# A one-core decoder step: where the near keys are copied, how wide the dense matmuls are, and how the weights lie

## The chip, the core and the metric

The kernel runs on one core of a Trainium2 chip. Its engines are TensorE (PE, with its weight loads as PEld), VectorE (DVE), ScalarE (ACT), GpSimd (POOL) and SyncE (SP); the last mainly issues DMAs, which all run on the core's 16 DMA engines. The metric is the device time of one launch in microseconds (us); arranging the inputs on the host before the launch is not in it.

## What is computed

One layer of a hybrid decoder, in float32, for a prompt of 1024 tokens and for 8 sequences of 8 new tokens (64 sample tokens) that have a cache of 2048 keys and values each:

```python
h = rmsnorm(x, norm_mix)
proj = h @ w_in                          # 1024 -> 3592 columns
a = gated_delta_rule(conv(proj[q, k, v]))     # 4 heads, with gates from 8 columns of w_in
b = dilated_window_attention(proj[q, k, v])   # 8 heads; sample tokens read the cache
x = x + concat(norm(a) * silu(z), norm(b)) @ w_out
h = rmsnorm(x, norm_ffn)
x = x + (silu(h @ w_gate) * (h @ w_up)) @ w_down     # width 2816
y = rmsnorm(x, norm_final)
```

Besides y it returns new states and caches. new_wk_sample is the key cache of each sequence, moved on by 8 rows: 2040 old rows and 8 new ones, 8 x 4 MB.

## The kernel before

Every dense product is made of three matmuls: each operand is split into a high part (ACT copies it, L223) and a low part (DVE subtracts, L224), and hi x hi, lo x hi and hi x lo are added in PSUM. wload (L226) fetches 512 KB of a weight on SP's queue into one of two raw buffers (WB = 2), wsplit makes whi and wlo, of which there are three each (WL = WH = 3), or, with own, four pairs in another pool. dense_T (L309) makes 128 output columns of all tokens, 24 matmuls per chunk of tokens; nat_mm (L1153) keeps 128 tokens in place and streams the weight.

The tokens come in two halves: F = 0 has four tiles of 128 prompt tokens, F = 1 has four more and the 64 sample tokens. The work is written as generators that yield an estimate of PE time, and beside() deals out the instructions of a main generator and of a side one by these; a scheduler then orders each engine's instructions by priority and readiness, and every queue runs in its order. keep_in_program_order pins a DMA behind the previous instruction of its queue.

The order of the stages is: norm and w_in projections (proj_a, proj_b) with the delta rule beside them; attention over the first half, outproj_a, and the first two pairs of decode_k; then the first half's outproj_b, ffn_norm and ffn(0) as the main work ("dense"), beside them attn(1), decode_k for the last two pairs, and decode_v; then outproj_b(1), ffn_norm(1) and ffn(1) with far_rows beside, which copies the far values in HBM (1536 KB each).

What the change touches: at the start (L1412 to L1417) two x tiles are loaded, then the table of constants (with the identity that the transposes use), the weight wmix, the first w_in weight, and three x tiles. Weights are sliced from their row-major arrays, so a 128-column weight tile arrives in pieces of 512 bytes, a 256-column one in pieces of 1 KB. Inside decode_k, at L1026, POOL's queue copies the last 512 keys of a sequence from cache to output, 1 MB. outproj_b works in four slices of 256 columns, one weight tile each. ffn takes its hidden blocks nb at a time (4, and 2 at f = 0 of F = 1 and at f = 20 of F = 0), gate and up by dense_T in chunks of tokens (512 for F = 0; 288 and 288 for F = 1), then the down projection: for F = 0 in four slices of 256 columns, for F = 1 in two of 512.

Of the kernel before, what the change touches and what calls it, by code (L numbers as in the profile page):

```python
# [86 lines left out]
def consts():  # L87

    p = np.arange(128)[:, None]
    c = np.arange(128)[None, :]  # L90
    c64 = np.arange(64)[None, :]
    c8 = np.arange(8)[None, :]
    t = {}
    t["ident"] = p == c
    t["ii"] = (p % 64) == (c % 64)
    t["utri"] = p <= c
    t["ones"] = np.ones((128, 128))
    t["maskT"] = np.where(c >= p, 0.0, NEG)
# [24 lines left out]
    ln = logn(count(d))  # L123
    wb = np.stack([np.where(d >= 0, -s * d, 0.0) + ln for s in slopes]).astype(np.float32)

    tt = (np.arange(128)[:, None] % 64) // 8
    sl = slopes[np.arange(128) % 8][:, None]
    x = np.arange(512)[None, :]
    dist = np.concatenate([
        np.broadcast_to(2048 - 16 * np.arange(96)[None, :], (128, 96)),  # L130
        512 + tt - 4 * (x % 128) - x // 128,
        tt - np.arange(8)[None, :]], axis=1)
    db_all = (np.where(dist >= 0, -sl * dist, 0.0) + logn(count(dist))).astype(np.float32)

    cc = np.arange(8)[None, :, None]
    rr = np.arange(32)[None, None, :]
    xin = (rr == cc + 8 * (np.arange(128)[:, None, None] % 4)).astype(np.float32).reshape(128, 256)
    return off, {"table": table, "wb": wb, "dbias": np.ascontiguousarray(db_all), "xin": xin}


def laid_out(cache_k):

    k = cache_k[0, :, PAST - 512:].reshape(DB, 128, 4, 4, 128)
    return np.ascontiguousarray(k.transpose(0, 4, 3, 2, 1).reshape(DB, 128, 4, 512))


def body(tc, I, O, C, off):
# [25 lines left out]
    ident, ii, utri, ones = K("ident"), K("ii"), K("utri"), K("ones")  # L173
# [52 lines left out]
    def wload(src, k, n):  # L226
        raw = wp.tile([128, k, n], F32, name="wraw", tag="wraw", bufs=WB)
        sp.dma_start(raw, src)
        return raw

# [89 lines left out]
    w_in = I["w_in"].rearrange("o (k p) n -> p (o k) n", p=128)  # L320
# [3 lines left out]
    def in_cols(i):  # L324
        return w_in[:, :, i * 128:(i + 1) * 128]
# [16 lines left out]
    def proj_a(G, tp, tb, hi, lo, ready={}):  # L342
# [38 lines left out]
        sp.dma_start(raw, w_in[:, :, 2048:2056])  # L381
# [35 lines left out]
    def proj_b(G, tp, hi, lo):  # L417

        W = GW[G]
        for kind in range(4):  # L420
            for j in range(4):
                c0_ = 2056 + kind * 512 + j * 128 if kind < 3 else 1536 + j * 128
                w = wsplit(w_in[:, :, c0_:c0_ + 128], 8, 128)
# [567 lines left out]
    def decode_k(tp, pairs, kb=2, kt_=3, qb=2, pb=1):  # L991
# [23 lines left out]
        for pi in pairs:  # L1015
            S = tp.tile([96, 2, 64], F32, name="S", tag="S", bufs=1)
            pa = obank()
            for s in range(2):
                b = 2 * pi + s
                c16, o16, c4, o4, src = cache_rows(I["cache_win_k"], O["new_wk_sample"], b)  # L1020
                for j in range(4):
                    for i in range(2):
                        hs = slice(i * 64, i * 64 + 64)
                        nc.gpsimd.tensor_copy(qbd[hs, s, j, 2 * j + i::8], qf[hs, j, b * 8:(b + 1) * 8])
                n = PAST - 512
                pool_q.dma_start(O["new_wk_sample"][0, b, n - DS:PAST - DS].rearrange("(a e) h d -> a (e h d)", a=64),  # L1026
                                 I["cache_win_k"][0, b, n:PAST].rearrange("(a e) h d -> a (e h d)", a=64))
# [117 lines left out]
    w_g = I["w_gate"].rearrange("o (k p) n -> p (o k) n", p=128)  # L1145
    w_u = I["w_up"].rearrange("o (k p) n -> p (o k) n", p=128)
    w_d = I["w_down"].rearrange("o (k p) n -> p (o k) n", p=128)
# [72 lines left out]
    def outproj_b(F, tp, x2):  # L1220
# [11 lines left out]
        for c in range(4):  # L1232
            w = wsplit(w_out[:, 4:8, c * 256:(c + 1) * 256], 4, 256)
            for i, rows, col in toks(F):
                ps = mbank()[:, :256]
                nat_mm(his(hi), his(lo), w, 4, rows, col, ps, True, True)
                xv = x2[:, col // 128, c * 256:(c + 1) * 256]
                dve.tensor_tensor(xv, ps, xv, op=OP.add)  # L1238
                yield 1.3
# [21 lines left out]
    def ffn(F, tp, x2, hp):  # L1261
        cols = [(0, 288), (288, 288)] if F else [(0, 512)]
# [19 lines left out]
        while f < nf:  # L1282
# [3 lines left out]
            for j in range(nb):  # L1286
                wg = wsplit(w_g[:, :, (f + j) * 128:(f + j + 1) * 128], 8, 128)
                wu = wsplit(w_u[:, :, (f + j) * 128:(f + j + 1) * 128], 8, 128)
                for c0, n in cols:
                    pg = yield from dense_T(*wg, hi, lo, c0, n)  # L1290
                    pu = yield from dense_T(*wu, hi, lo, c0, n)
                    th = hp.tile([128, 512], F32, name="hth", bufs=2)[:, :n]
                    act.activation(th, pg[:, :n], AF.Tanh, scale=0.5)  # L1293
                    dve.scalar_tensor_tensor(th, th, 1.0, pg[:, :n], op0=OP.add, op1=OP.mult)
                    dve.tensor_tensor(th, th, pu[:, :n], op=OP.mult)
                    act.activation(hh[j][:, c0:c0 + n], th, AF.Copy, scale=0.5)
                    m = min(n, 512 - c0)
                    dve.scalar_tensor_tensor(hl[j][:, c0:c0 + m], th[:, :m], 0.5, hh[j][:, c0:c0 + m].bitcast(F32),
                                             op0=OP.mult, op1=OP.subtract)
                    if m < n:  # L1300
                        dve.scalar_tensor_tensor(hh[j][:, 576:640], th[:, m:n], 0.5, hh[j][:, 512:576].bitcast(F32),
                                                 op0=OP.mult, op1=OP.subtract)
                yield 0.1
            last, wide = f + nb == nf, F or nb == 2
            ncol = 512 if wide else 256
            parts = nb * ncol // 1024

            def weights(c):

                k = nb // parts  # L1310
                return [wsplit(w_d[:, f + q * k:f + (q + 1) * k, c * ncol:(c + 1) * ncol], k, ncol, own=hp if F else None)
                        for q in range(parts)]
# [25 lines left out]

    def far_rows(c, o, new):
# [5 lines left out]
        sp.dma_start(o[0, :, PAST - DS:PAST].rearrange("b t h d -> b t (h d)"), new.rearrange("(b t) f -> b t f", t=DS))  # L1345

# [66 lines left out]
    sp.dma_start(tab, C["table"])  # L1413
    wbc = bcast_row(npl, I["norm_mix"], "wmix")
    raws = [(i, wload(in_cols(i), 8, 128)) for i in IN_ORDER[:E1]]
    x0 += load_in(0, npl, range(2, 5))
    raws += [(i, wload(in_cols(i), 8, 128)) for i in IN_ORDER[E1:E2]]  # L1417
# [51 lines left out]
    dense = Side(outproj_b(0, hp, x2), ffn_norm(0, hp, x2), ffn(0, hp, x2, hp))  # L1469
    with ExitStack() as s1:  # L1470
# [9 lines left out]
    with ExitStack() as s1:  # L1480
        dv = Side(decode_v(pool(s1, "dv", "right")), ahead=O6)
        beside(dense, (dv, R8), until=U5)
        dv.run()
    op = pool(st1, "h1", "right")
# [39 lines left out]
```

## Time and profile before

| | us |
|---|---|
| runs, median of 3 | 1784.57 |
| lowest and highest run | 1784.05 and 1786.42 |
| the profiled execution, its own time | 1786.49 |
| its span, first to last instruction | 1784.7 |
| PE busy | 1697.0 |
| DVE busy | 1150.2 |
| ACT busy | 679.4 |

The profile is of one execution. In the timeline a row is one instruction or several merged ones: start, duration, engine, line, operation, out<-in, count, and in brackets how long the engine was idle before it and what ended that. A busy PE is not PE at its peak: the ends of matmuls are modelled and overlap, so the cost of one in a run is read from start to start. The granted clock of PE is given as a share of 2.4 GHz; its lower level is 1.2.

### The profile page before, as it was taken

Reading aid. Unit: us, or ns where it says so; the run is one execution under the profiler, and the core shown is the slowest. Engines: PE = TensorE matmul, PEld = TensorE weight load, DVE = VectorE, ACT = ScalarE, POOL = GpSimd, SP = SyncE. Lnnn points to the kernel's source line nnn. Section 1 sums busy time; section 2 is a strip of 40 time slices with the busy share of each in tenths; the row PEclk is TensorE's granted clock in tenths of the full one; section 3 lists DMA queues with packets and bytes.
Section 4 is the critical chain, followed back from the end, with each engine's and each line's share of the span. In section 5 each row is a group of like instructions: output and inputs, shape, how many; then the busy total and the mean of one; then the engine's idle time right before and its main releaser. Section 6 shows DMA issues by size and latency. Waiting matters only on the chain. (4 is left out here: it accounts for less than half of the span.)

```text
span 1784.7 us, 27958 instructions
## 1 busy us (share of the span) xinstructions
PE 1697.0 (95%) x10462; PEld 1464.7 (82%) x10462; DVE 1150.2 (64%) x2829; ACT 679.4 (38%) x1379; POOL 78.2 (4%) x200
## 2 busy tenths in 40 slices
PE   4999999997999999999999989999998999999997
PEld 4988789996766668878887778888887999999996
DVE  6978966866776757797666546676576444343435
ACT  4545434441423353676421134454234223131222
POOL 1000000001001000000011001111100000000000
PEclk9999999998999999999998999999998999999999
DMA  8645556468898867534299678798494333241321
GB/s 272 182 145 159 162 179 171 116 200 271 266 282 256 256 208 225 188 104 118 66 284 287 180 224 256 248 304 274 133 325 154 128 95 95 59 130 36 107 72 65
DMA packets 309569, 324.96 MB, mean 182 GB/s; under 512 B 28221, under 2 KB 260669, under 8 KB 307754
## 3 DMA queue, kind: packets, MB, share of 16 engines
q1 hardware_dynamic: 297754, 275.64, 51.6%
q0 software_dynamic: 10304, 43.08, 6.8%
q10 hardware_dynamic: 1376, 4.46, 0.7%
q8 instruction: 82, 1.34, 0.3%
q14 instruction: 53, 0.43, 0.1%
HBM read 251.31 MB, written 105.63 MB: 200 GB/s over the span
## 5 line engine op out<-in xcount | busy, mean ns | idle before, releaser
L198 PE MATMUL pm<-act_hi,whi 128*128 128x288 f32 (+1 forms) x1056 | 349.4, 331 | 0.2 <-ACT act_hi L223 0.2
L198 PE MATMUL pm<-act_lo,whi 128*128 128x288 f32 (+1 forms) x1056 | 348.1, 330 | 0.0
L198 PE MATMUL pm<-act_hi,wlo 128*128 128x288 f32 (+1 forms) x1056 | 347.4, 329 | 0.0
L223 ACT ACTIVATE whi<-wraw 128x1024 fp32r<-128x1024 f32 x182 | 192.8, 1059 | 381.8 <-PE pm L198 275.8
L224 DVE TENSOR_TENSOR wlo<-wraw,whi 128x1024 fp32r<-128x1024 f32 x182 | 222.3, 1222 | 123.8 <-ACT whi L223 123.3
L198 PE MATMUL pm<-xh,whi 128*128 128x320 f32 (+2 forms) x672 | 230.6, 343 | 11.5 <-ACT whi L223 8.6
L198 PE MATMUL pm<-xl,whi 128*128 128x320 f32 (+2 forms) x672 | 228.4, 340 | 0.1
L198 PE MATMUL pm<-xh,wlo 128*128 128x320 f32 (+2 forms) x672 | 226.7, 338 | 0.2
L198 PEld LDWEIGHTS pm<-act_hi,whi 128*128 128x128 f32 x1056 | 199.2, 189 | 18.4 <-issue 2.1
L198 PEld LDWEIGHTS pm<-act_hi,wlo 128*128 128x128 f32 x1056 | 199.3, 189 | 14.5 <-issue 0.5
L198 PEld LDWEIGHTS pm<-act_lo,whi 128*128 128x128 f32 x1056 | 199.3, 189 | 14.2 <-issue 0.2
L198 PEld LDWEIGHTS pm<-xh,whi 128*128 128x128 f32 x672 | 129.1, 192 | 25.9 <-ACT whi L223 9.1
L1320 DVE TENSOR_TENSOR x<-pm,x 128x256 f32<-128x256 f32 (+1 forms) x148 | 79.9, 543 | 98.2 <-PE pm L198 97.8
L198 PEld LDWEIGHTS pm<-xl,whi 128*128 128x128 f32 x672 | 129.0, 192 | 11.9 <-issue 3.2
L198 PEld LDWEIGHTS pm<-xh,wlo 128*128 128x128 f32 x672 | 128.7, 192 | 10.6 <-DVE wlo L224 1.5
L198 PE MATMUL pm<-own,hh 128*128 128x512 f32 x440 | 129.4, 390 | 0.0
L198 PE MATMUL pm<-whi,hh 128*128 128x256 f32 (+1 forms) x336 | 101.6, 303 | 12.9 <-DVE x L1320 7.6
L198 PE MATMUL pm<-whi,hl 128*128 128x256 f32 (+1 forms) x336 | 99.7, 299 | 0.0
L198 PE MATMUL pm<-wlo,hh 128*128 128x256 f32 (+1 forms) x336 | 99.4, 297 | 0.0
L198 PEld LDWEIGHTS pm<-own,hh 128*128 128x128 f32 x440 | 82.2, 188 | 16.9 <-issue 0.2
L198 PE MATMUL pm<-whi,nat_hi 128*128 128x256 f32 x288 | 83.4, 293 | 1.5 <-DVE n_ss L219 1.1
L1293 ACT ACTIVATE hth<-pm 128x288 f32<-128x288 f32 (+1 forms) x66 | 30.5, 462 | 139.4 <-PE pm L198 139.3
(362 smaller groups left out, 3180.9 us busy)
## 6 DMA issues: line engine op xcount, KB each, us to landing
wraw<-w_in SPq DMA_DIRECT2D x56, 512.0 KB, 4.6
wraw<-w_gate SPq DMA_DIRECT2D x44, 512.0 KB, 3.7
wraw<-w_up SPq DMA_DIRECT2D x44, 512.0 KB, 3.8
wraw<-w_down SPq DMA_DIRECT2D x44, 512.0 KB, 3.6
new_wk_sample<-cache_win_k SPq DMA_DIRECT2D x8, 1536.0 KB, 8.2
qbc<-smp SPq DMA_DIRECT2D x32, 384.0 KB, 7.2
kt<-cache_win_k SPq DMA_DIRECT2D x32, 384.0 KB, 7.0
vt<-cache_win_v SPq DMA_DIRECT2D x32, 384.0 KB, 4.2
```

The costliest lines, as they stand in the source:

```text
L198: pe.matmul(out, lhsT, rhs, start=start, stop=stop)
L223: act.activation(hi, src, AF.Copy)
L224: dve.tensor_sub(lo, src, hi.bitcast(F32))
L1293: act.activation(th, pg[:, :n], AF.Tanh, scale=0.5)
L1320: dve.tensor_tensor(xv, ps, xv, op=OP.add)
```

## The change

The near keys are no longer copied in decode_k. wload now takes one entry of a list after each weight load, when there is one, and issues it on SP's queue: a copy of 256 rows (512 KB), pinned behind the load. The list of 16 copies is set just before the dense work of the first half begins, and what is left of it is issued when that work's side generators are done. The identity leaves the table and gets a tensor of its own; at the start wmix, the identity, the first weight and the last three x tiles come ahead of the table. w_in, w_gate, w_up and w_down are laid out on the host so that each weight tile is one block with 4 KB per partition; w_out stays. outproj_b and the down projection of F = 0 work in two slices of 512 columns, with two weight tiles of 256 rows each per slice. The second FFN takes its tokens as 256 and 320, and in its first step goes through both hidden blocks for the first 256 tokens before it comes to the other 320; the second block's weights lie in the own buffers.

```diff
-    t["ident"] = p == c
...
+def lay_out(a):
+
+    a = dict(a)
+    a["w_ba"] = np.ascontiguousarray(a["w_in"][0][:, 2048:2056].reshape(8, 128, 8).transpose(1, 0, 2))
+    a["w_in"] = blocks_of(a["w_in"], IN_COLS)
+    for k in ("w_gate", "w_up"):
+        a[k] = blocks_of(a[k], range(0, FF, 128))
+    a["w_down"] = np.ascontiguousarray(a["w_down"][0].reshape(11, 2, 128, 2, 512).transpose(0, 3, 2, 1, 4))
+    return a
...
-    ident, ii, utri, ones = K("ident"), K("ii"), K("utri"), K("ones")
+    ident = cp.tile([128, 128], F32, name="ident")
+    ii, utri, ones = K("ii"), K("utri"), K("ones")
...
     def wload(src, k, n):
         raw = wp.tile([128, k, n], F32, name="wraw", tag="wraw", bufs=WB)
         sp.dma_start(raw, src)
+        move()
         return raw
+
+    moves = iter(())
+
+    def move():
+
+        x = next(moves, None)
+        if x is not None:
+            tc.keep_in_program_order(sp.dma_start(*(y.rearrange("s h d -> s (h d)") for y in x)))
+        return x
...
     def in_cols(i):
-        return w_in[:, :, i * 128:(i + 1) * 128]
+        return I["w_in"][i]
...
-        sp.dma_start(raw, w_in[:, :, 2048:2056])
+        sp.dma_start(raw, I["w_ba"])
...
-                c0_ = 2056 + kind * 512 + j * 128 if kind < 3 else 1536 + j * 128
-                w = wsplit(w_in[:, :, c0_:c0_ + 128], 8, 128)
+                w = wsplit(I["w_in"][12 + kind * 4 + j], 8, 128)
...
-                n = PAST - 512
-                pool_q.dma_start(O["new_wk_sample"][0, b, n - DS:PAST - DS].rearrange("(a e) h d -> a (e h d)", a=64),
-                                 I["cache_win_k"][0, b, n:PAST].rearrange("(a e) h d -> a (e h d)", a=64))
                 for r in range(0, 512, 256):
                     kaT = tp.tile([128, 4, 256], F32, name="kaT", bufs=kb)
                     sp.dma_start(kaT, C["near_kT"][b, :, :, r:r + 256])
...
-        for c in range(4):
-            w = wsplit(w_out[:, 4:8, c * 256:(c + 1) * 256], 4, 256)
+        for c in range(2):
+            cs = slice(c * 512, (c + 1) * 512)
+            w = [wsplit(w_out[:, k:k + 2, cs], 2, 512) for k in (4, 6)]
             for i, rows, col in toks(F):
-                ps = mbank()[:, :256]
-                nat_mm(his(hi), his(lo), w, 4, rows, col, ps, True, True)
-                xv = x2[:, col // 128, c * 256:(c + 1) * 256]
+                ps = mbank()
+                for q in range(2):
+                    nat_mm(his(hi), his(lo), w[q], 2, rows, col, ps, q == 0, q == 1, 2 * q)
+                xv = x2[:, col // 128, cs]
                 dve.tensor_tensor(xv, ps, xv, op=OP.add)
-                yield 1.3
...
     def ffn(F, tp, x2, hp):
-        cols = [(0, 288), (288, 288)] if F else [(0, 512)]
+        cols = [(0, 256), (256, 320)] if F else [(0, 512)]
...
-            for j in range(nb):
-                wg = wsplit(w_g[:, :, (f + j) * 128:(f + j + 1) * 128], 8, 128)
-                wu = wsplit(w_u[:, :, (f + j) * 128:(f + j + 1) * 128], 8, 128)
-                for c0, n in cols:
-                    pg = yield from dense_T(*wg, hi, lo, c0, n)
-                    pu = yield from dense_T(*wu, hi, lo, c0, n)
...
+
+            early = F and f == 0
+            ws = {}
+            for j, (c0, n) in ([(j, c) for c in cols for j in range(nb)] if early else [(j, c) for j in range(nb) for c in cols]):
+                if j not in ws:
+                    ws = ws if early else {}
+                    ws[j] = [wsplit(I[x][f + j], 8, 128, own=hp if early and j else None) for x in ("w_gate", "w_up")]
+                wg, wu = ws[j]
+                pg = yield from dense_T(*wg, hi, lo, c0, n)
+                pu = yield from dense_T(*wu, hi, lo, c0, n)
+                th = hp.tile([128, 512], F32, name="hth", bufs=2)[:, :n]
...
-            last, wide = f + nb == nf, F or nb == 2
-            ncol = 512 if wide else 256
+            last, ncol = f + nb == nf, 512
             parts = nb * ncol // 1024
 
             def weights(c):
 
-                k = nb // parts
-                return [wsplit(w_d[:, f + q * k:f + (q + 1) * k, c * ncol:(c + 1) * ncol], k, ncol, own=hp if F else None)
-                        for q in range(parts)]
+                return [wsplit(I["w_down"][f // 2 + q, c], 2, 512, own=hp if F else None) for q in range(parts)]
...
+    def move_all(m):
+        nonlocal moves
+        while move() is not None:
+            pass
+        moves = m
...
+    def rows_of(i, o, first, last, n):
+
+        for b in range(DB):
+            for r in range(first, last, n):
+                yield O[o][0, b, r - DS:r - DS + n], I[i][0, b, r:r + n]
...
     x0 = list(load_in(0, npl, range(2)))
-    sp.dma_start(tab, C["table"])
     wbc = bcast_row(npl, I["norm_mix"], "wmix")
+    sp.dma_start(ident, C["ident"])
     raws = [(i, wload(in_cols(i), 8, 128)) for i in IN_ORDER[:E1]]
     x0 += load_in(0, npl, range(2, 5))
+    sp.dma_start(tab, C["table"])
     raws += [(i, wload(in_cols(i), 8, 128)) for i in IN_ORDER[E1:E2]]
...
     dense = Side(outproj_b(0, hp, x2), ffn_norm(0, hp, x2), ffn(0, hp, x2, hp))
+    move_all(rows_of("cache_win_k", "new_wk_sample", PAST - 512, PAST, 256))
     with ExitStack() as s1:
         at1 = Side(attn(1, pool(s1, "at", "right"), **A1), ahead=O4)
         beside(dense, (at1, R7), until=U3)
...
         beside(dense, (dv, R8), until=U5)
         dv.run()
+    move_all(iter(()))
     op = pool(st1, "h1", "right")
...
     arrays = {k: np.ascontiguousarray(np.asarray(v)) for k, v in inputs.items()}
+    arrays = lay_out(arrays)
```

## Rows read from the trace of the kernel before

**Rows 1.** The page: busy time of each engine.

```profile
PE 1697.0 (95%) x10462; PEld 1464.7 (82%) x10462; DVE 1150.2 (64%) x2829; ACT 679.4 (38%) x1379; POOL 78.2 (4%) x200
```

**Rows 2.** Windows: busy us of each engine (instructions), granted clock, DMA share, GB/s.

```profile
0.00:35.00 35.00, 11.29 (x61) 9.88 (x62) 19.16 (x71) 13.52 (x24) 2.41 (x8) 0.98 0.86 297
405.00:450.00 45.00, 36.33 (x187) 29.12 (x187) 29.26 (x97) 8.40 (x21) 5.11 (x20) 0.88 0.87 271
785.00:905.00 120.00, 118.46 (x747) 102.55 (x746) 90.16 (x236) 61.37 (x116) 3.66 (x17) 1.00 0.39 113
905.00:1000.00 95.00, 88.17 (x451) 70.58 (x450) 61.70 (x77) 18.07 (x22) 11.93 (x32) 0.91 0.96 280
1305.00:1350.00 45.00, 35.52 (x266) 33.22 (x266) 36.67 (x105) 16.17 (x24) 0.00 (x0) 0.90 0.87 309
1440.00:1485.00 45.00, 45.00 (x262) 40.62 (x261) 16.99 (x26) 7.69 (x12) 0.00 (x0) 1.00 0.21 59
```

**Rows 3.** Timeline, 0 to 20 us, POOL's and SP's queues: start, us, instruction.

```profile
1.30 1.68 POOL L1026 DMA_DIRECT2D new_wk_sample<-cache_win_k  x3
3.24 11.22 SPq L334 DMA_DIRECT2D xt<-x_prompt  x2
```

**Rows 4.** Timeline, 0 to 20 us, DVE and PE; in brackets the idle time before.

```profile
8.10 0.16 DVE L219 SCALAR_TENSOR_TENSOR n_ss<-n_ss 128x1 f32<-128x1 f32 x1
17.23 1.28 DVE L289 SCALAR_TENSOR_TENSOR xn<-xt,n_ss,wmix 128x1024 f32<-128x1024 f32 x1 [8.97 <-DMA wmix<-norm_mix]
18.57 1.76 PE L294 MATMUL pn<-tab,xn 128*128 128x128 f32 x7 [18.57 <-DVE xn L289]
```

**Rows 5.** The page, DMA issues: count, KB each, median us to landing.

```profile
wraw<-w_gate SPq DMA_DIRECT2D x44, 512.0 KB, 3.7
wraw<-w_down SPq DMA_DIRECT2D x44, 512.0 KB, 3.6
new_wk_sample<-cache_win_k SPq DMA_DIRECT2D x8, 1536.0 KB, 8.2
```

**Rows 6.** Timeline of SP and ACT, 830 to 860 us.

```profile
833.70 0.37 SPq L228 DMA_DIRECT2D wraw<-w_down  x1
843.28 1.06 ACT L223 ACTIVATE whi<-wraw 128x1024 fp32r<-128x1024 f32 x1 [0.50 <-PE pm L198]
```

**Rows 7.** Timeline of PE: first and last of 93 and of 36 rows.

```profile
1311.67 0.28 PE L198 MATMUL pm<-wlo,nat_hi 128*128 128x256 f32 x1
...
1322.51 0.28 PE L198 MATMUL pm<-wlo,nat_hi 128*128 128x256 f32 x1
1286.10 0.39 PE L198 MATMUL pm<-act_hi,whi 128*128 128x512 f32 x1
...
1294.03 0.39 PE L198 MATMUL pm<-act_hi,wlo 128*128 128x512 f32 x1
```

**Rows 8.** Groups by form: count, busy us, mean ns, idle before and for whom.

```profile
L198 PE MATMUL pm<-whi,hh 128*128 128x256 f32 x320 | 94.8, 297 | 12.8 <-DVE x L1320 7.6 <-DVE hth L1295 5.2
L224 DVE TENSOR_TENSOR wlo<-wraw,whi 128x1024 fp32r<-128x1024 f32 x182 | 222.3, 1222 | 123.8 <-ACT whi L223 123.3
```

**Rows 9.** Timeline of DVE and PE, 1340 to 1360 us, and a window.

```profile
1344.98 1.28 DVE L224 TENSOR_TENSOR act_lo<-pn,act_hi 128x512 fp32r<-128x512 f32 x2
1349.83 0.85 PE L198 MATMUL pm<-act_hi,whi 128*128 128x288 f32 x2
1353.40 0.59 PE L198 MATMUL pm<-act_hi,whi 128*128 128x288 f32 x1
1340.00:1350.00 10.00, 3.88 (x17) 3.31 (x18) 9.51 (x27) 5.13 (x9) 0.00 (x0) 0.56 0.44 157
```

**Rows 10.** Timeline of PE at two holes; DVE's longest waits, 940 to 1070 us.

```profile
439.38 0.80 PE L198 MATMUL pm<-xh,whi 128*128 128x512 f32 x1 [8.63 <-ACT whi L223]
959.64 0.58 PE L198 MATMUL pm<-whi,hh 128*128 128x256 f32 x1 [3.95 <-DVE hth L1295]
DVE pr L1000 <- DMA kt<-cache_win_k: 12.2, 4, 3.7
```

More of the change, by code (lines that the diff above doesn't have):

```diff
@@ L137, in consts @@
     xin = (rr == cc + 8 * (np.arange(128)[:, None, None] % 4)).astype(np.float32).reshape(128, 256)
-    return off, {"table": table, "wb": wb, "dbias": np.ascontiguousarray(db_all), "xin": xin}
+    return off, {"table": table, "ident": (p == c).astype(np.float32), "wb": wb, "dbias": np.ascontiguousarray(db_all), "xin": xin}
 def laid_out(cache_k):
@@ L144, in laid_out, with blocks_of @@
     return np.ascontiguousarray(k.transpose(0, 4, 3, 2, 1).reshape(DB, 128, 4, 512))
+def blocks_of(w, cols):
+    return np.ascontiguousarray(np.stack([w[0][:, c:c + 128].reshape(8, 128, 128).transpose(1, 0, 2) for c in cols]))
+IN_COLS = [i * 128 for i in range(12)] + [2056 + i * 128 for i in range(12)] + [1536 + i * 128 for i in range(4)]
+def lay_out(a):
[6 more added lines that the diff above has]
+    return a
 def body(tc, I, O, C, off):
@@ L318, in dense_T @@
         return ps
-    w_in = I["w_in"].rearrange("o (k p) n -> p (o k) n", p=128)
     ba = [None, None]
     def in_cols(i):
-        return w_in[:, :, i * 128:(i + 1) * 128]
+        return I["w_in"][i]
     COLS = ([(0, 256), (256, 320)], [(0, 512)])
@@ L1144, in body @@
     w_out = I["w_out"].rearrange("o (k p) n -> p (o k) n", p=128)
-    w_g = I["w_gate"].rearrange("o (k p) n -> p (o k) n", p=128)
-    w_u = I["w_up"].rearrange("o (k p) n -> p (o k) n", p=128)
-    w_d = I["w_down"].rearrange("o (k p) n -> p (o k) n", p=128)
     def toks(F):
@@ L1231, in outproj_b @@
             yield 1.5
-        for c in range(4):
-            w = wsplit(w_out[:, 4:8, c * 256:(c + 1) * 256], 4, 256)
+        for c in range(2):
+            cs = slice(c * 512, (c + 1) * 512)
+            w = [wsplit(w_out[:, k:k + 2, cs], 2, 512) for k in (4, 6)]
             for i, rows, col in toks(F):
-                ps = mbank()[:, :256]
-                nat_mm(his(hi), his(lo), w, 4, rows, col, ps, True, True)
-                xv = x2[:, col // 128, c * 256:(c + 1) * 256]
+                ps = mbank()
+                for q in range(2):
+                    nat_mm(his(hi), his(lo), w[q], 2, rows, col, ps, q == 0, q == 1, 2 * q)
+                xv = x2[:, col // 128, cs]
                 dve.tensor_tensor(xv, ps, xv, op=OP.add)
-                yield 1.3
+                yield 2.6
     def join(tp, x2, zero):
@@ L1285, in ffn @@
             hl = [hp.tile([128, 512], F32R, name="hl", tag="hl", bufs=6) for _ in range(nb)]
-            for j in range(nb):
-                wg = wsplit(w_g[:, :, (f + j) * 128:(f + j + 1) * 128], 8, 128)
-                wu = wsplit(w_u[:, :, (f + j) * 128:(f + j + 1) * 128], 8, 128)
-                for c0, n in cols:
-                    pg = yield from dense_T(*wg, hi, lo, c0, n)
-                    pu = yield from dense_T(*wu, hi, lo, c0, n)
[L1292 to L1298, printed above, removed]
+            early = F and f == 0
@@ new lines, in ffn @@
+            ws = {}
[7 more added lines that the diff above has]
+                th = hp.tile([128, 512], F32, name="hth", bufs=2)[:, :n]
+                act.activation(th, pg[:, :n], AF.Tanh, scale=0.5)
+                dve.scalar_tensor_tensor(th, th, 1.0, pg[:, :n], op0=OP.add, op1=OP.mult)
+                dve.tensor_tensor(th, th, pu[:, :n], op=OP.mult)
+                act.activation(hh[j][:, c0:c0 + n], th, AF.Copy, scale=0.5)
+                m = min(n, 512 - c0)
+                dve.scalar_tensor_tensor(hl[j][:, c0:c0 + m], th[:, :m], 0.5, hh[j][:, c0:c0 + m].bitcast(F32),
+                                         op0=OP.mult, op1=OP.subtract)
+                if m < n:
+                    dve.scalar_tensor_tensor(hh[j][:, 576:640], th[:, m:n], 0.5, hh[j][:, 512:576].bitcast(F32),
```

3 lines of the change are left out of this document (removed).

## The prediction

> **What bounds the kernel now.** I read the page first: TensorE (PE) is busy 95% of the span [rows 1]. So time can only come from two places: from holes in PE's row, or from PE's own work. To find the holes I cut the span into windows [rows 2]. Three kinds stand out. In the first 35 us PE works 11.29 us while the DMA engines are 86% busy. From 405 to 450 it works 36.33 us and from 905 to 1000 88.17 of 95, with the DMA engines at 87% and 96%. From 1305 to 1350 it works 35.52 us and VectorE (DVE) 36.67. Between them lies the stretch into which the copies go: at 785 to 905 PE is full and the DMA engines are only 39% busy. In the second FFN (1440 to 1485) PE has no hole, so nothing but its own work counts there.
>
> **The start, and the copies.** In the code the eight near-key copies (L1026) sit inside decode_k, far down. The timeline of GpSimd's queue (POOL) shows where they really run: they wait for nothing, so three of them, 1 MB each, are issued at 1.30 us, before any weight [rows 3]. On SP's queue the table stands ahead of wmix in the code, and the two x tiles behind the first weight hold the queue for 11.22 us [rows 3]. What that costs is one row: DVE finishes the statistics at 8.10 + 0.16 = 8.26 us, then idles 8.97 us until wmix has landed; its xn at 17.23 releases PE's first instruction at 18.57 [rows 4]. After the change only 1 MB of x lies ahead of wmix. At the 297 GB/s of the first 35 us [rows 2], 1.5 MB take 5 us; even with 3 us on top for the way to the first byte (my estimate: nearly a whole w_gate load, 3.7 us [rows 5]) wmix is there by 8, with the statistics. So xn starts at 8.26 and the whole chain moves up by 8.97 us. I take **-9.0**. It could be -12 if the later loads of this stage, freed of 3 MB (3 / 0.297 = 10 us of DMA time), also let the chain behind 20 us close up; it could be -6 if that chain, where DVE works 19.16 of 35 us and most of it behind 17 [rows 2, 4], resists. The other five copies run at 43 to 55 and 148 to 158 us, where the page's PE slices show no hole; I count them at nothing.
>
> The copies come back as 16 pieces of 512 KB on SP's queue, each pinned behind one weight load, from the first weight of outproj_b(0) on: 4 loads there, 8 gate/up and 4 w_down of the first block, so up to about 870 us. Behind each piece wait the next weight load and the loads of attn. A 1536 KB copy lands in 8.2 us [rows 5], so a piece takes some 2.7 us of the engines. The cover: a weight lands some 3.6 us after its issue (the one of 833.70 at about 837.3), and the next split comes at 843.28, 9.6 us after the issue and released by PE, not by a DMA [rows 5, 6]. So there are at least 6 us to spare for 2.7. The 8 MB fill 16 x 2.7 = 43 of the 61% x 120 = 73 us that the DMA engines stand idle [rows 2]. I take **0**, up to +8 if half of the pieces cost 1 us in attn's own loads.
>
> **Wider matmuls in outproj_b and the first FFN's down projection.** 320 x 3 matmuls of 256 columns (hh, hl) become 480 of 512, and of outproj_b's 416 (4 slices of 4 x 12 and of 4 x 12 + 8) come 208: 688 pairs become one each. Start to start, 93 rows of 256 columns take (1322.51 - 1311.67) / 92 = 117.8 ns, and 36 of 512 take (1294.03 - 1286.10) / 35 = 226.6 [rows 7]. A pair saves 9.0 ns: 688 x 9.0 = 6.2 us. DVE adds half as often, and PE waited 12.8 us before these groups, 7.6 of them for such an add [rows 8]; a small piece, 1 us, should go. Together **-7**, between -6 and -14.
>
> Against it: a slice now needs two weight tiles (two wsplits) at once out of three split buffers. The fourth tile of a block can be split only when the first is released, 6 matmuls before the slice ends, and is needed 6 matmuls into the next one: 12 x 0.227 = 2.7 us later. Its split is 1.06 us on ScalarE (ACT) and 1.22 on DVE, 2.3 in all [rows 6, 8]. If two foreign instructions of 1.2 us stand ahead, that is 2.0 us of stall, at 7 places (5 blocks, 2 outproj_b): +14 at worst, 0 at best. Between the groups PE has the side work of attn and decode, which gives the split time; I take **+2**.
>
> The Trainium skill has a rule that speaks against this gain: the page TensorE: Matmul & The Clock Gate, section Back-to-back issue gap, gives an isolated gap of N / 2.4 + 2.5 ns, so a pair would save 2.5 ns and this term would be 1.7 us instead of 6.2. The rows show some 11 to 13 ns above N / 2.4 at both widths, so I stay with them.
>
> **Columns 256 and 320 in the second FFN.** Between 256 and 512 columns a column costs (226.6 - 117.8) / 256 = 0.425 ns [rows 7]. As both are lines on that slope, 288 + 288 and 256 + 320 cost the same: **0**; if 288 lay 1 ns off the line, 1056 pairs would make 2 us of it, up or down.
>
> **Entry into the second FFN.** The first 256 columns need token tiles 0 and 1 only, and their turn for both blocks of weights now comes first. In the trace the second half of tile 1 is split at 1344.98 to 1346.26; PE gets two matmuls in at 1349.83 before it waits again, and only from 1353.40 does it run on [rows 9]. The order of the change lets PE start at 1346.3, 7.1 us earlier, of which some 3 were filled already (16 transposes at the lower clock, a few matmuls). But the second block's two splits, 2 x 1.22 us of DVE, are now due in the same stretch, where DVE is 9.51 of 10 us busy [rows 9]. 7.1 - 3 - about 1 that is not hidden: **-3**, between -7 and 0.
>
> **Weights by tiles.** Loads of 512 KB land after 3.7 us in 512-byte pieces (w_gate) and 3.6 in larger ones (w_down) [rows 5], so in stretches with room the layout is worth nothing. Where the engines are full it frees time: 59 GB/s at a share of 0.21 is 281 GB/s at a full share, 309 at 0.87, where large copies run, is 355 [rows 2]; 524 KB take 1.87 or 1.48 us. From 905 to 1000, at a share of 0.96, some 9 such loads run (one in 10 us, as in [rows 6]): 3.5 us. PE's waits there, the longest 3.95 us at 959.64, stand behind DVE, which waited at pr for kt's loads (12.2 us in four waits) [rows 10]; the granted clock over the stretch is 0.91 [rows 2]. I take **-4**, between -14 (88.17 of 95 busy, and the clock) and +2 (wider groups crowd DVE). The 8.63 us hole at 439.38 stands behind a split that waited for its weight [rows 10], in a queue of waiting DMAs; the change leaves these where they are: **0**, from -9 to +5.
>
> The Trainium skill's page DMA: Bandwidth & Descriptors, section Specifications, puts line rate at transfers of 512 bytes and more; by that the layout would free nothing and the sum would be some 3 us later. Windows of mixed traffic do not refute it, so that lies inside the range.
>
> **Sum.** -9 + 0 - 7 + 2 + 0 - 3 - 4 + 0 = -21 us. The profiled execution took 1786.49 us with a span of 1784.7; the median of the runs is 1784.57. 1786.49 - 21 = 1765.5 by the profile; the runs lie 1.9 lower: **1763.6 us**.
>
> **Rivals.** (a) Deeper: the holes at 439 and 959 and their like close as well, with the clock that follows them, since all hang on crowded DMA engines. For it: 87 to 98% share. Against it: the bytes there stay. Price -9 and -10: 1745. Chance 0.13. (b) The split buffers bind: +14 instead of +2: 1776. For it: 2.7 us against 2.3; against it: side work between groups. Chance 0.13. (c) PE's time goes by columns alone, and widening gives no more than the 1 us of waits: 1770. Against it: [rows 7]. Chance 0.03. (The gap rule of the page named above comes to nearly this.) (d) The change doesn't do what it says at the start: wmix still lands late, since something else stands in the queue, and only 3 us come: 1770. Chance 0.05. (e) Slower: each of the 16 pieces on SP's queue delays the weight load behind it by its full 2.7 us, and PE waits that long: 16 x 2.7 = 43 us, 1807. It decides once a weight has less than 2.7 us between its landing and its split; the rows show about 6. Chance 0.06. The forecast itself, 1755 to 1773: 0.60.
>
> **Range and chances.** 1745 to 1777 leaves out (e) and the outer parts of (a) and (b), some 0.15. A measurement of this kernel can tell about 0.2%, 3.6 us, from no change. Faster by more: 0.60 + 0.13 + 0.12 + 0.03 + 0.04 = 0.92, cut to 0.90 for a reordering of queues that I can't see; same 0.03; slower 0.07.
>
> **What would show it.** Start: the first transpose near 9.6 us and no L1026 on POOL. Copies: 16 issues between about 750 and 880, no wait of ACT for wraw there. Widening: 227 ns steps in the first FFN; a wait of PE for whi or wlo at a slice's second half speaks for (b). Entry: the first act_hi matmul right behind tile 1. Decode: the waits of DVE at pr shorter by some us. The forecast falls if a new hole of over 5 us opens in front of a weight of the first FFN, or if the start moves by under 6.

## The result, and the profile after

| | us |
|---|---|
| before, median of the runs beside | 1784.31 |
| after, median of 4 runs (1800.55 to 1811.69) | 1809.01 |
| ratio, with its 95% interval | 1.0128, 1.0094 to 1.0162 |
| profiled execution of after, its span | 1806.6 |

The change is slower by 1.3%; the forecast was 1763.6, 1745 to 1777. The page of after, the line of busy times that answers [rows 1], and the windows that answer [rows 2]:

```profile
PE 1708.4 (95%) x9774; PEld 1433.9 (79%) x9774; DVE 1149.8 (64%) x2771; ACT 678.3 (38%) x1379; POOL 75.8 (4%) x192
0.00:35.00 35.00, 18.92 (x101) 17.38 (x102) 24.81 (x86) 17.33 (x30) 0.72 (x5) 0.90 0.62 212
785.00:905.00 120.00, 102.98 (x529) 83.78 (x528) 77.48 (x204) 57.55 (x113) 0.53 (x1) 0.92 0.35 117
905.00:1000.00 95.00, 83.87 (x347) 63.76 (x345) 51.67 (x68) 20.38 (x26) 9.01 (x24) 0.93 0.67 208
```

PE has the 688 instructions less that were counted (10462 to 9774), and the first 35 us are as hoped. But from 785 to 905 us, where PE had been full, it is now busy 103 of 120 us at a granted clock of 0.92, with the DMA engines only 35% busy. Followed through the trace by PE's instructions: the last matmul of attention over the first half (po from pt) stands at 671.6 us, 5.6 earlier than before (677.2); the last one of attn(1) (po from ph or pl) at 908.5, 26.3 later (882.2). So 32 us go in 240 us, beside outproj_b(0) and the first FFN.

What PE waited for from 700 to 1000 us in after (line, releaser: us in total, times, longest):

```profile
PE ps L217 <- ACT qh L242: 7.2, 3, 3.1
PE pa L927 <- DVE pl L243: 6.1, 9, 0.9
PE pm L217 <- DVE wlo L243: 5.8, 5, 2.8
PE pm L217 <- DVE hth L1322: 2.8, 1, 2.8
PE pm L217 <- ACT whi L242: 2.2, 2, 2.0
```

There is no long hole; the longest wait has 3.1 us. PE waits now for splits of weights, now for splits of attention. None of these splits had itself waited for a DMA; of the waits listed only the one for hth, at 989 us, stands behind such a wait (DVE's pr, 8.6 us for kt). The rows of the longest wait show where it comes from and what it costs beyond itself: SP's load of q, ACT's and PE's timeline in after, and PE's granted clock behind it (window: us, then busy us of PE, PEld, DVE, ACT, POOL, clock, DMA share, GB/s):

```profile
829.50 1.19 SPq L885 DMA_DIRECT2D q<-qs  x2
843.23 0.38 ACT L242 ACTIVATE ph<-pa 128x256 fp32r<-128x256 f32 x1 [6.52 <-PE pa L927]
848.02 0.62 ACT L242 ACTIVATE qh<-q 128x512 fp32r<-128x512 f32 x1
848.75 0.47 PE L217 MATMUL ps<-kst,qh 128*128 128x512 f32 x1 [3.13 <-ACT qh L242]
849.50:856.00 6.50, 6.01 (x16) 4.70 (x17) 3.95 (x13) 2.03 (x5) 0.00 (x0) 0.50 0.00 0
```

The load of q was issued at 829.50; ACT stood idle for 6.52 us until 843.23, behind an instruction that waited for PE, and split q only at 848.02. After PE had stood still for 3.13 us the granted clock was at its lower level of 1.2 GHz (0.50) for the next 6.5 us. The same matmuls take longer then and count as busy, so a part of the loss hides in the first line of the page (19.6 of 49.1 us, by the account under e6).

### The profile page after: what moved, and what is told of

Its sections match the earlier page's. It is cut to its first block, busy times and chain, and to the rows that moved or that the text cites. A ratio compares the mean times of both kernels' runs of the same rounds, so it can differ in the third digit from the quotient of the medians.

```text
span 1806.6 us, 26518 instructions
## 1 busy us (share of the span) xinstructions
PE 1708.4 (95%) x9774; PEld 1433.9 (79%) x9774; DVE 1149.8 (64%) x2771; ACT 678.3 (38%) x1379; POOL 75.8 (4%) x192
## 4 chain that ended last, share of the span: by engine, by line
PE 66%; DVE 8%; DMA 5%; issue 2%; ACT 2%; SPq 0%; DVEq 0%; ACTq 0%
PE pm L217 49%; PE po L217 6%; PE pg L217 3%; DMA kt<-cache_win_k 3%; PE ps L217 2%; PE pa L927 2%; PE pc L217 1%; DVE wlo L243 1%; PE pa L217 1%; DVE pl L243 1%; DMA wraw<-w_up 1%; DMA y_prompt<-xn 1%; PE pn L1199 1%; DMA Pd<-pd 1%; ACT whi L242 0%
## 5 line engine op out<-in xcount | busy, mean ns | idle before, releaser
L217 PE MATMUL pm<-act_hi,whi 128*128 128x512 f32 (+2 forms) x1024 | 341.4, 334 | 6.3 <-DVE hth L1321 2.9
L217 PE MATMUL pm<-act_hi,wlo 128*128 128x512 f32 (+2 forms) x1024 | 339.9, 332 | 1.8 <-DVE wlo L243 1.8
L217 PE MATMUL pm<-act_lo,whi 128*128 128x512 f32 (+2 forms) x1024 | 340.4, 332 | 0.2 <-DVE act_lo L243 0.2
L217 PEld LDWEIGHTS pm<-act_hi,wlo 128*128 128x128 f32 x1024 | 194.3, 190 | 17.5 <-DVE wlo L243 2.4
L1344 DVE TENSOR_TENSOR x<-pm,x 128x512 f32<-128x512 f32 x108 | 74.2, 689 | 105.8 <-PE pm L217 105.6
L1320 ACT ACTIVATE hth<-pm 128x256 f32<-128x256 f32 (+2 forms) x66 | 30.5, 462 | 141.9 <-PE pm L217 141.8
L1322 DVE TENSOR_TENSOR hth<-hth,pm 128x256 f32<-128x256 f32 (+2 forms) x66 | 35.0, 530 | 69.4 <-PE pm L217 69.2
L217 PE MATMUL pm<-whi,nat_hi 128*128 128x256 f32 (+1 forms) x216 | 71.0, 333 | 6.4 <-ACT whi L242 3.8
L243 DVE TENSOR_TENSOR vl<-vt,vh 96x1024 fp32r<-96x1024 f32 (+1 forms) x48 | 58.4, 1219 | 26.3 <-ACT vh L242 26.2
L217 PE MATMUL pm<-whi,hh 128*128 128x512 f32 x176 | 71.5, 409 | 3.7 <-ACT whi L242 2.0
```

The costliest lines, as they stand in the source:

```text
L217: pe.matmul(out, lhsT, rhs, start=start, stop=stop)
L243: dve.tensor_sub(lo, src, hi.bitcast(F32))
```

## The experiments

Unless said otherwise each is after with the edit shown. Times are medians of 3 to 9 runs, beside before on the same chip, whose median there was 1784 to 1789 us; ratios are to that, with 95% intervals. Two theories stood at first: M, the pieces on SP's queue cost the time; W, the slices of 512 columns with two weight tiles each do.

**e1, no pieces.** The list of pieces is never set, so those rows are not written.

```diff
-    move_all(rows_of("cache_win_k", "new_wk_sample", PAST - 512, PAST, 256))
```

> The changed kernel without the 16 copies of the last keys; these rows of new_wk_sample are left out. Theory M (the pieces on SP's queue cost the 35 us lost between 750 and 910 us): 1768 to 1780 us, attention beside the first FFN ends near 875. Theory W (the slices of 512 columns with two weight tiles, and the coarser turns between main and side work, cost it): still 1798 to 1810 us.

Measured: 1760.21 us, ratio 0.9851 (0.98 to 0.9902).

**e2, the copies on POOL again.** As e1, with the eight copies of 1 MB back in decode_k.

```diff
+                n = PAST - 512
+                pool_q.dma_start(O["new_wk_sample"][0, b, n - DS:PAST - DS].rearrange("(a e) h d -> a (e h d)", a=64),
+                                 I["cache_win_k"][0, b, n:PAST].rearrange("(a e) h d -> a (e h d)", a=64))
```

> The changed kernel with the copies back on GpSimd's queue inside decode_k, where they run at the start. M: the start loses its 8 to 10 us again and the stretch 750 to 910 is as before: 1776 to 1788 us. W: start and stretch both lost: 1808 to 1820 us.

Measured: 1759.9 us, 0.9846 (0.9815 to 0.9876), with all of the output. Both times lie far below the ranges of W, and below those of M too.

**e3, narrow slices.** outproj_b and the down projection of F = 0 in 256 columns again, pieces kept.

> The changed kernel with outproj_b and the first FFN's down projection in four slices of 256 columns again, the pieces kept on SP's queue. M: nothing won back, and 6 us of matmul time added: 1805 to 1818 us. W: 1775 to 1785 us.

Measured: 1818.21 us, 1.0174 (1.0144 to 1.0204). W is out: the wide slices gain. Page of e3, its busy times and one group:

```profile
PE 1714.5 (94%) x10462; PEld 1473.7 (81%) x10462; DVE 1155.3 (64%) x2829; ACT 679.1 (37%) x1379; POOL 75.7 (4%) x192
L218 PE MATMUL pm<-wlo,hh 128*128 128x256 f32 x320 | 92.8, 292 | 5.5 <-DVE wlo L244 5.5
```

PE is busy 6.1 us longer than in after, at nearly the same mean clock (0.978 and 0.977).

**e4, the pieces beside the second FFN.** The list is set just before ffn(1), where the DMA engines are a quarter busy.

> The changed kernel with the list of pieces set just before the second FFN, so that they go behind its weight loads, where the DMA engines are 20 to 40% busy. M: 1768 to 1782 us. W: 1798 to 1812 us.

Measured: 1809.01 us, 1.014 (1.0086 to 1.0195). The cost moves along with the pieces, some 49 us at either place. ACT's timeline there:

```profile
1370.40 1.06 ACT L242 ACTIVATE whi<-wraw 128x1024 fp32r<-128x1024 f32 x1 [3.81 <-DMA wraw<-w_gate]
1386.20 0.38 ACT L1320 ACTIVATE hth<-pm 128x256 f32<-128x256 f32 x1 [14.73 <-PE pm L217]
1386.48 1.05 ACT L242 ACTIVATE whi<-wraw 128x1024 fp32r<-128x1024 f32 x1
```

This was the first sight of the cause. ACT stands idle for 14.73 us, though the load of the weight that it splits at 1386.48 was issued at 1375.11. The split stands in ACT's order behind hth of the block before, so it can't start before PE has finished that block; then it starts without a wait for its weight, and PE waits for the split (ACT whi 12.0 us in 7 waits from 1366 to 1466). The idle time alone is no sign: in e1 ACT stands idle for 13.71 us ahead of the like hth, but there the split behind it waits 2.50 us more for PE to free a buffer, and PE waits for no split of a weight from 1310 to 1420. That the order is what cost e4 its time is not shown by a run of its own; what follows is on after.

From here on the theories were O, the cost is the order in which the scheduler puts each engine's instructions when the pieces are among them, and D, rival (e) of the prediction, a piece delays the weight behind it. The orders differ: place by place in the traces of e1 and after, leaving the pieces aside, another kind of instruction (by operation, tiles and shape) stands at 209 of ACT's 1379 places, at 432 of 2771 on DVE, at 975 of 9774 on PE and at 118 of 716 on SP. (The expectations from e7 on count displaced instructions in another way, and no trace shows their numbers.) So the order was held, by edges that give order alone: each instruction as it is written down in the program (T) comes behind the one that stands ahead of it on its engine in another build (a holds these places, engine by engine, with -1 between them).

```diff
+    T = [i for i in tc.nc.cur_bb.bb.instructions if i.name not in PIECES]
+    for p, q in zip(a[:-1], a[1:]):
+        if p >= 0 and q >= 0:
+            tc.add_manual_dep(T[q], T[p].name, mybir.DependencyInfo(mybir.DependencyClass.NoSync, mybir.DependencyReason.DATA), reason="order")
```

**e5, pieces, in the order of the kernel without.**

> After with its 16 pieces behind the weight loads, but with the instructions of PE, DVE, ACT, POOL and SP held, by edges that give order alone and add no wait, to the order in which they stand in the kernel without pieces (1760 us). Theory O (what the pieces cost is the order that the scheduler lays out around them, with each weight's split behind other work of ACT and DVE, while the DMA engines are in time): about 1760, at most 1770. Theory D, rival (e) of the prediction (a piece holds the next weight back in the queue or on the DMA engines): about 1805, since the same 8 MB go through the same queue at the same weights.

Measured: 1756.72 us, 0.9834 (0.9805 to 0.9863).

**e6, no pieces, in the order of after.**

> The reverse: no pieces (those rows of the output are left out), but the instructions of each engine held to the order in which they stand in after. Theory O: 1800 to 1810, as slow as after though not one byte of the copies moves. Theory D: about 1760, as the kernel without pieces.

Measured: 1805.95 us, 1.0121 (1.0086 to 1.0157). O holds from both sides: 16 pieces in the good order cost nothing, and the order of after without one byte of them is as slow as after. The traces show that the orders were held: leaving the copies aside, e5 has at every place of PE, DVE, ACT, POOL and SP the same kind of instruction as e1, and e6 the same as after. They also show where the loss sits. PE's order is the same in after and e5 up to 691 us of after and again from 1004 us. At the first point after is 2.5 us behind e5, at the second 49.0, and at the end 49.1. The same work, in after, e5 and e6:

```profile
691.10:1003.70 312.60, 272.40 (x1379) 217.89 (x1379) 201.07 (x468) 129.97 (x240) 9.84 (x26) 0.94 0.52 168
688.50:954.70 266.20, 253.49 (x1381) 206.62 (x1380) 199.81 (x472) 128.45 (x240) 9.45 (x27) 0.99 0.62 198
690.40:1003.30 312.90, 272.69 (x1380) 218.36 (x1379) 201.61 (x469) 130.23 (x240) 10.04 (x26) 0.94 0.46 143
```

Two windows at fixed times, of e6, then of e5:

```profile
785.00:905.00 120.00, 102.84 (x531) 83.40 (x532) 78.11 (x206) 58.02 (x114) 0.53 (x1) 0.93 0.27 82
905.00:1000.00 95.00, 83.91 (x346) 63.67 (x345) 52.27 (x68) 20.61 (x27) 9.20 (x24) 0.93 0.65 200
```

```profile
785.00:905.00 120.00, 118.58 (x651) 98.13 (x651) 88.43 (x216) 59.86 (x114) 5.01 (x18) 1.00 0.49 154
905.00:1000.00 95.00, 94.29 (x416) 70.69 (x415) 66.34 (x76) 21.58 (x27) 11.96 (x32) 1.00 0.97 298
```

e6 repeats after's PE to 0.2 us in both windows. e5 has the fuller DMA engines (0.49) and the fuller PE. What the orders do is seen at the raw weight tile from 700 to 900 us, in after and then in e5 (the splits, what ACT and DVE waited for ahead of them, and the time from load to landing):

```profile
L242 ACT ACTIVATE whi<-wraw x11: 1044/1052/1084, 704.0 to 898.3; 128x1024 fp32r<-128x1024 f32 x11
  PE pm L217: 2.5, 1
DMA to landing us min/median/max: 3.4/5.1/6.1
```

```profile
L242 ACT ACTIVATE whi<-wraw x17: 1044/1061/1063, 701.6 to 898.1; 128x1024 fp32r<-128x1024 f32 x17
  PE pm L217: 22.5, 11
DMA to landing us min/median/max: 4.1/5.5/5.6
```

The loads land alike, and as late in the fast kernel as in the slow one. But in e5 eleven of ACT's 17 splits stand at the head of its queue and wait only for PE to free a buffer, so a weight is split as early as there is room; in after one of 11 does, and nine of the others come with no idle time of ACT ahead of them, behind other work. The queue of SP says the same: what it waited for from 670 to 900 us, after and e5:

```profile
SPq L874 <- DVE mx L912: 51.2, 5, 21.0
SPq L247 <- DVE wlo L243: 11.6, 2, 6.4
```

```profile
SPq L247 <- DVE wlo L243: 61.2, 14, 9.5
SPq L874 <- DVE mx L909: 10.6, 3, 5.2
```

In e5 it is weights (L247) that stand at the head, waiting for a free raw tile; in after it is attention's wb (L874), waiting for DVE, and what stands behind it in the queue waits along. And on PE the turns are coarser. Counted over 700 to 880 us, PE changes between dense work (pm) and other work, mostly attention, 361 times in e5 and 113 times in after and in e6. Timeline of PE, after and e5:

```profile
841.57 0.39 PE L217 MATMUL pm<-act_lo,whi 128*128 128x512 f32 x1
841.79 0.39 PE L217 MATMUL pm<-act_hi,wlo 128*128 128x512 f32 x1
842.02 0.39 PE L217 MATMUL pm<-act_hi,whi 128*128 128x512 f32 x1
842.25 0.39 PE L217 MATMUL pm<-act_lo,whi 128*128 128x512 f32 x1
```

```profile
839.81 0.28 PE L217 MATMUL po<-pl,vst 128*128 128x256 f32 x1
839.92 0.40 PE L217 MATMUL pm<-act_lo,whi 128*128 128x512 f32 x1
840.16 0.28 PE L217 MATMUL po<-ph,vst 128*128 128x256 f32 x1
840.27 0.40 PE L217 MATMUL pm<-act_hi,wlo 128*128 128x512 f32 x1
```

In e5 a dense matmul fills the time in which attention's next operand is split, and the other way round; in after the one comes when the other is done. Accounts: the spans differ by 1806.6 - 1757.5 = 49.1 us. PE is busy 1708.4 and 1688.8 us for the same 9774 instructions, 19.6 more at a mean granted clock of 0.977 against 0.985, and its idle time, 98.2 and 68.7, makes the other 29.5. Of this, 46.4 us lie in the stretch of the three windows above, 18.9 of them in busy time.

**e7, small pieces.** 16 of the 256 rows of each. No order is held, in e8 neither.

```diff
-            tc.keep_in_program_order(sp.dma_start(*(y.rearrange("s h d -> s (h d)") for y in x)))
+            tc.keep_in_program_order(sp.dma_start(*(y[:16].rearrange("s h d -> s (h d)") for y in x)))
```

> After with the 16 pieces pinned at the same places but a sixteenth of their bytes, 32 KB each (the other rows are left out). No order is held: on ACT 59 of 1188 instructions stand elsewhere than without pieces, where after has 232. Theory D by bytes: 16 x 0.2 = 3 us above 1760, so 1763. A fixed price for each DMA on the queue: up to 1808. Theory O: a quarter of the loss at most, 1760 to 1772.

**e8, pieces on POOL's queue.**

```diff
-            tc.keep_in_program_order(sp.dma_start(*(y.rearrange("s h d -> s (h d)") for y in x)))
+            tc.keep_in_program_order(pool_q.dma_start(*(y.rearrange("s h d -> s (h d)") for y in x)))
```

> After with the same 16 pieces of 512 KB traced behind the same weight loads, but issued by POOL's queue, each in POOL's program order. On ACT 37 of 1188 instructions stand elsewhere than without pieces. Theory O: 1760 to 1770. Theory D by SP's queue: also 1760. Theory D by the DMA engines (the bytes collide with the weights wherever they are issued): 1790 to 1808, if the pieces run between 680 and 920 us.

Measured: e7 1746.65 us, 0.9777 (0.9752 to 0.9802), better than no pieces at all and below every range; e8 1775.52, 0.9924 (0.9897 to 0.9951). e7 has one more order, and a lucky one. e8 missed what O expected, and its trace shows D at work. Its POOL and ACT timelines:

```profile
688.76 3.89 POOL L257 DMA_DIRECT2D new_wk_sample<-cache_win_k  x8 [0.18 <-issue]
722.80 1.06 ACT L242 ACTIVATE whi<-wraw 128x1024 fp32r<-128x1024 f32 x1 [23.92 <-DMA wraw<-w_out]
```

POOL's queue doesn't wait for SP's loads, so all 16 pieces go out from 688.76 to 707 us as one burst, and a w_out load issued at 693.74 lands at 722.7. PE waited 24.0 us in one piece for attention's ph, which stands behind that split on ACT. So D is real for 8 MB at once; with the pieces spaced by weight loads, as in e5, no such wait is seen.

**e9, all pieces at full size, in the order of e7.**

> After with all its 16 pieces at full size, and each engine's instructions held to the order in which they stand in the kernel with the small pieces (1746.65 us). Theory O: about 1747 to 1752, since only the order counts and 8 MB fit beside the first FFN. Theory D: at least 10 us more than the small pieces, 1757 to 1795.

Measured: 1752.8 us (1743.99 to 1757.38), 0.9802 (0.9773 to 0.9832), with all of the output. By the ratios the full pieces cost 0.25% over e7, with intervals that overlap; of the 9.4 us between the two spans, 4.7 are there at 676 us, before the first piece. This is the lowest ratio of a kernel here that does all the work.

**e10 to e12, one or two engines held** to the order of the kernel without pieces, the others laid out anew by the scheduler: ACT and DVE in e10, SP in e11, PE in e12.

> After with its pieces; only ACT's and DVE's instructions are held to the order of the kernel without pieces, PE and SP are laid out anew around them (689 of PE's 9047 and 83 of SP's 726 stand elsewhere than without pieces). If the loss sits in where the splits and the other work of ACT and DVE stand: 1755 to 1770. If it sits in SP's or PE's order: 1780 to 1808.

> After with its pieces; only SP's instructions (the order in which loads are issued) are held to the order of the kernel without pieces; ACT, DVE and PE are laid out anew (275 of ACT's 1188 stand elsewhere, 695 of DVE's 2773). If the loss sits in ACT's and DVE's order: 1780 to 1808, as after. If it sits in the order of the loads (k, q and wb of attn and the weights): 1755 to 1770.

> After with its pieces; only PE's instructions are held to the order of the kernel without pieces (89 of ACT's and 267 of DVE's stand elsewhere). If ACT's and DVE's order follows PE's closely enough: 1755 to 1770; if the splits still stand late on ACT: 1780 to 1808.

Measured: 1798.4, 1798.79 and 1813.29 us (1.0064, 1.0065 and 1.015). Neither the order of ACT and DVE, nor that of SP, nor that of PE gives the time back by itself, and e12 lies above both of its ranges. As the other engines are laid out anew each time, these runs don't tell on which engine the order of after is bad. The clearest case is e10; what ACT waited for from 690 to 790 us:

```profile
ACT whi L242 <- DMA wraw<-w_out: 32.5, 2, 23.1
```

There the splits stand early on ACT, as in e5, but SP issues the third w_out load only at 720.73, behind other DMAs of its queue, three of which waited 3 to 6 us each for DVE, and ACT waits 23.1 us for it with attention's work behind. A good order of one engine among others that don't fit it is a new wait. In e12 PE changes between dense and other work 313 times from 700 to 880 us, and yet it is as slow as after, so fine turns on PE are not enough either.

**e13 to e15, single terms, with the order of the kernel without pieces held on all engines.** e13 is e5 again; e14 has no pieces but the copies on POOL; e15 has the weights in their old layout.

> After with its 16 pieces and each engine held to the order of the kernel without pieces, as the kernel that the two others of this call are compared with: 1753 to 1760.

> The same order on each engine, but no pieces: the eight copies of 1 MB stand on POOL's queue again, three of them at about 1.3 us. If the start's 9 us (first term of the sum) reach the end: 9 us more than the held kernel with pieces, 1762 to 1769. If the stretch of the decode, where the DMA engines are 97% busy, eats them: 0 to 4 us more.

> The held kernel with pieces, same order on each engine, but w_in, w_gate, w_up and w_down loaded from their old layout, in 512-byte and 2 KB runs, and not by tiles. The forecast took 4 us for the layout, with bounds of 14 less and 2 more: so 1757 to 1764. If transfers of 512 bytes go at the full rate: no change, 1753 to 1760.

Measured: e13 1754.82 us (0.9836, 0.9805 to 0.9867), e14 1763.22 (0.9869, 0.9848 to 0.989), e15 1756.88 (0.9835, 0.9811 to 0.9858). The copies at the start cost 8.4 us by the medians and some 6 by the ratios, and the two intervals overlap; the layout is worth 0 to 2 us, within the spread. In e1 and e2, whose order is the same but for six places on PE, the start made no difference in the medians, but e1's three runs spread over 12 us. Instruction by instruction e14 is 9.0 us behind e13 at the first transpose and 8.0 at the end, and e2 is 9.0 and 3.8 behind e1.

## Why the prediction was wrong, and where it was right

**The pieces: 0, up to +8. This step failed; measured 1809 against 1755 to 1760, some +50 us.** Its reasoning about the DMAs was sound: a weight landed in time behind a piece in after and e5 alike, and from 690 to 910 us no split on ACT waited over 0.3 us for its load in after. The term by itself, e5 against e1 in the same order, is 3.5 us less in the medians, with intervals that overlap, and in the traces 0.9 us more over the stretch of the pieces. The sign that I named for it, no wait of ACT for wraw, was indeed seen there, and it said nothing; the other sign, 16 issues between 750 and 880 us, was not: they run from 674.6 to 917.5 us in after. What failed is the unspoken step between: that the instructions around the pieces stay where they were. The six spare microseconds [rows 5, 6] were read from the order of before, in which the split is already at the head of its engine when PE frees the buffer. In after it no longer is. (The six were also misread: the split at 843.28 is that of the load before, and the weight of 833.70 is split at 853.6, 19.9 us after its issue.) The text took 0.02 off its chance "for a reordering of queues that I can't see", and gave that no price.

**Rival (e)** said 1807, which is nearly the time, by a mechanism that e5 and e6 rule out: with the same pieces at the same loads PE does not wait, and without them it does. A forecast that hits by another mechanism would have sent the mending to the wrong place: fewer or smaller transfers, and not the order.

**The start: -9, right at the start; 4 to 8 of it reach the end (e1 and e2, e13 and e14).** The first transpose comes at 8.96 us in after (forecast near 9.6) and 18.57 before [rows 4]:

```profile
8.96 1.97 PE L323 MATMUL pn<-ident,xn 128*128 128x128 f32 x8 [8.96 <-DVE xn L318]
```

One part was told apart by e14: wmix is issued at 1.65 us on SP's queue there too, and still

```profile
16.73 1.28 DVE L318 SCALAR_TENSOR_TENSOR xn<-xt,n_ss,wmix 128x1024 f32<-128x1024 f32 x1 [9.12 <-DMA wmix<-norm_mix]
1.31 1.68 POOL L1053 DMA_DIRECT2D new_wk_sample<-cache_win_k  x3
```

So the three copies hold wmix up, whatever the order of the first loads on SP; loads by need alone bring 0.5 us of this (first transpose at 18.07).

**The wider matmuls: -7, right.** e3 against after makes 6.1 us of PE's busy time for 688 pairs, 8.9 ns each, where 9.0 were taken from [rows 7], and 1818.2 against 1809.0 in the medians, with intervals that overlap a little; as no order was held, some of these 9 us may be order. The gap rule of the Trainium skill (TensorE: Matmul & The Clock Gate, Back-to-back issue gap), 2.5 ns a pair, would have made 1.7 of it; the rows decide against it. **The split buffers: +2, measured near 4, at one place of seven; rival (b), +14, refuted.** In e5 PE's idle time before the group whi,hh of 512 columns is 1.1 us and before wlo,hh none, so the five blocks are clean. In outproj_b(1) PE waits 3.93 us for a split, which stands on ACT behind the store of a block that DVE has not made yet:

```profile
L217 PE MATMUL pm<-whi,hh 128*128 128x512 f32 x176 | 70.8, 402 | 1.1 <-DVE hth L1322 1.1
1302.33 2.00 ACT L242 ACTIVATE whi<-wraw 128x1024 fp32r<-128x1024 f32 x2 [4.20 <-DVE xn L1300]
1303.44 0.79 PE L217 MATMUL pm<-whi,nat_hi 128*128 128x512 f32 x1 [3.93 <-ACT whi L242]
```

The same wait is in after, e9 and e13 (3.8 to 4.0 us), and not in before.

**Columns 256 and 320: 0, right.** In the second FFN a turn from one down projection to the next takes 76.3 us in before (1520.7 to 1597.0) and 76.4 in after (1542.4 to 1618.8). **Entry: -3, too small.** From the last matmul of outproj_b(1) to the third down projection go 184.2 us in before (1336.5 to 1520.7), 175.2 in after (1367.2 to 1542.4) and 175.8 in e5: 8.4 to 9.0, beyond the end of 7 that was given, so the time was too small even without the subtraction for work "filled already". What the rest is, no run shows.

**The layout: -4, mis-sized.** It brought 0 to 2 us. The median load of w_gate takes 5.2 us to land in e15 and 4.1 in e13 (lines of the page), one of w_in 4.3 and 4.4, so where something is freed, the time doesn't show it. The sign, shorter waits of DVE at pr, was seen (from 900 to 1050 us 23.7 us before, 16.4 in e5), but with the old layout as well (17.2 in e15). By time the Trainium skill's rule that 512 bytes go at line rate (DMA: Bandwidth & Descriptors, Specifications) forecast the better figure, though the landing times are not equal. PE's gain from 905 to 1000 us, 88.17 [rows 2] to 94.29 in e5, is there with the old layout too:

```profile
905.00:1000.00 95.00, 93.78 (x411) 69.70 (x410) 66.22 (x76) 21.09 (x26) 12.19 (x32) 1.00 0.98 294
```

**The hole at 439 us: 0, right.** It stands at 428.46 us in after, with 7.77 us behind the same split.

Held in a good order the change is thus worth 1.6 to 2.0% (e5, e13, e9), some 30 us; while the terms other than the pieces made 21 in the forecast. Of the 9 between, the entry brought some 6 more, the layout 2 to 4 less, the start 1 to 5 less and the split buffers some 2 less; the rest, some 8 to 14, I put down to order without having shown it, since none of these orders is that of before.

Open stays what makes one order good. The number of displaced instructions does not: by the traces e4 has 56 on ACT and is as slow as after, with 209, while e8 has 71 and e7, the fastest, 101. Why the scheduler puts the splits late when pieces are among the loads is open too; the traces show only the order that came out.

## What to carry to other kernels

In a kernel whose engines are ordered by a scheduler, an inserted DMA that costs the chip nothing can cost 3% by what it does to the order of everything else, and an unrelated edit can gain some by the same (e7); so compare the built orders of both programs before reading the times, and hold the order when you price one edit. A split that waits on PE for a free buffer is early; one that runs as soon as its engine comes to it may be late, and PE then waits for it without any DMA in the row. Judge by the count (11 of 17 splits waited for PE in e5, 1 of 11 in after) and not by the age of the data: from issue to split a weight takes 5 to 29 us in after and 5 to 43 in e5. Copies of megabytes issued at once delay a load among them: three at the start held the first work up by 9 us, and in the middle a load took 29 us to land, while the same bytes in pieces behind the loads cost nothing that these runs can tell.

## What the runs showed of the hardware

Two things that I had not expected. The order alone moves the same work, all 16 pieces in it, between 1753 (e9) and 1813 us (e12), and 19.6 of the 49.1 us between e5 and after are not waits but longer busy time of TensorE, which ran at its lower level after waits such as the one of 3.13 us shown above (granted clock 0.94 in after and 0.99 in e5 over the same work). And 16 copies of 512 KB from HBM to HBM, spaced by weight loads, left the landing of those loads between 3.4 and 6.1 us, while the same 16 in one burst made a load that was issued among them take 29 us.
